# Weighting each token's row by two expert weights: input tiles of 22 tokens instead of 24, output tiles of half an input tile, and four-token VectorE products

## The chip, the cores and the metric

The kernel runs on one core of one Trainium2 chip. The metric is the device time of one execution in microseconds (us), the median of several runs. The profile is one execution recorded by the hardware profiler; its times are counted from the start of its span.

## What is computed

`x` holds 16 x 1024 = 16,384 tokens of 512 float32 values, `expert_weights` two float32 weights for each token. The output has, for each token, its row times the first weight and its row times the second. `expert_indices` is not used.

```
x_expanded = x[:, :, np.newaxis, :].repeat(k, axis=2)     # k = 2
weights = expert_weights[..., np.newaxis]
return (x_expanded * weights).astype(np.float32)
```

So 33.6 MB of `x` and 0.13 MB of weights are read and 67.1 MB are written, with one multiplication for each value written.

## The kernel before, in words

The 16,384 tokens are seen as 128 tokens for each of 128 partitions. `groups` cuts these 128 into input tiles of 24 tokens a partition five times and 8 once. In a tile of T tokens, partition p holds T neighbouring tokens, so its share of `x` is one contiguous run of T x 2 KB in memory and its share of the output one of T x 4 KB. One token a partition is 128 x 2 KB = 0.26 MB of `x` and 0.52 MB of output.

There are three pools: one tile for all the weights, two buffers for input tiles (`x_pool`, 48 KB a partition each) and two for output tiles (`o_pool`, 12 tokens, 48 KB a partition each).

- **Weights** (lines 53, 54 and 58): three transfers issued by SyncE (SP) at the start, for the first tile, the other four tiles of 24, and the last tile.
- **Loads** (`load`, line 82): issued on ScalarE's (ACT's) queue. Tile 0 comes in six pieces of 4 tokens, so that work can begin early; the others are one transfer each. `load(0)` and `load(1)` are issued before the loop; `load(i + 2)` stands behind the products of tile i, since it writes the buffer that they read.
- **Products** (lines 100 and 106): for each token and each of its two weights one instruction of 128 x 512 values. Of three successive ones, two run on VectorE (DVE, `tensor_scalar`, line 106) and one on ACT (`mul`, line 100).
- **Stores** (line 115): issued by SP when 12 tokens, one output tile of 6.29 MB, are multiplied; 11 stores in all, the last of 8 tokens. The output tile can be written again when its store has landed, so the products of one output tile wait for the store two before it.

The order on each engine is the order in the source. Waits are put in by the framework: a product waits for its input tile or piece and for its output buffer; a store on SP waits for the products of both engines; `load(i + 2)` on ACT's queue waits for DVE's products of tile i, and ACT's next products stand behind it. A transfer's packets are spread over the core's 16 DMA engines, 8 rows (partitions) of a tile to each engine; each row of a tile is one packet.

Of the kernel before, what the change touches and what calls it, by code (L numbers as in the profile page):

```python
# [1 line left out]

# [4 lines left out]


@with_exitstack
def kernel(  # L10
    ctx: ExitStack,
    tc: tile.TileContext,
    x: bass.AP,
    expert_indices: bass.AP,
    expert_weights: bass.AP,
    out: bass.AP,
):
    nc = tc.nc

    batch, seq, hidden = x.shape  # L20
    k = expert_weights.shape[-1]
    P = nc.NUM_PARTITIONS
    ntok = batch * seq
    assert ntok % P == 0
    A_TOTAL = ntok // P

    f32 = mybir.dt.float32
    row = k * hidden
    TX = 24
    TO = 12  # L30

    groups = [[24], [24], [24], [24], [24], [8]]
    assert sum(sum(g) for g in groups) == A_TOTAL

    xf = x.rearrange("b s h -> (b s) h")
    of = out.rearrange("b s k h -> (b s) (k h)")
    wf = expert_weights.rearrange("b s k -> (b s) k")

    w_pool = ctx.enter_context(tc.tile_pool(name="w_pool", bufs=1))
    x_pool = ctx.enter_context(tc.tile_pool(name="x_pool", bufs=2))  # L40
    o_pool = ctx.enter_context(tc.tile_pool(name="o_pool", bufs=2))

    w_tile = w_pool.tile([P, A_TOTAL * k], f32)

    def rows(of_all, done, T):
        return of_all[done * P : (done + T) * P, :].rearrange(
            "(p a) n -> p (a n)", a=T
        )

    T0 = sum(groups[0])  # L50
    G = len([g for g in groups[1:] if sum(g) == T0])
    head = (1 + G) * T0
    nc.sync.dma_start(out=w_tile[:, : T0 * k], in_=rows(wf, 0, T0))
    nc.sync.dma_start(
        out=w_tile[:, T0 * k : head * k].rearrange("p (g n) -> p g n", g=G),
        in_=wf[T0 * P : head * P, :].rearrange("(g p a) n -> p g (a n)", g=G, p=P),
    )
    nc.sync.dma_start(
        out=w_tile[:, head * k :], in_=rows(wf, head, A_TOTAL - head)
    )  # L60

    tiles = []
    done = 0
    for group in groups:
        T = sum(group)
        a0 = 0
        for n in group:
            tiles.append((done, T, a0, n))
            a0 += n
        done += T  # L70

    loaded = []

    def load(i):
        if i >= len(tiles):
            return
        done, T, a0, n = tiles[i]
        x_tile = x_pool.tile([P, TX * hidden], f32)
        src = rows(xf, done, T)
        step = TX // 6 if i == 0 else n  # L80
        for at in range(0, n, step):
            nc.scalar.dma_start(
                out=x_tile[:, at * hidden : (at + step) * hidden],
                in_=src[:, (a0 + at) * hidden : (a0 + at + step) * hidden],
            )
        loaded.append(x_tile)

    for i in range(2):
        load(i)
    for i, (done, T, a0, n) in enumerate(tiles):  # L90
        x_tile = loaded[i]
        outr = rows(of, done, T)
        for t in range(n):
            if t % TO == 0:
                o_tile = o_pool.tile([P, TO * row], f32)
            for kk in range(k):
                c = (done + a0 + t) * k + kk
                o = t % TO * row + kk * hidden
                if c % 3 == 2:
                    nc.scalar.mul(  # L100
                        out=o_tile[:, o : o + hidden],
                        in_=x_tile[:, t * hidden : (t + 1) * hidden],
                        mul=w_tile[:, c : c + 1],
                    )
                    continue
                nc.vector.tensor_scalar(  # L106
                    out=o_tile[:, o : o + hidden],
                    in0=x_tile[:, t * hidden : (t + 1) * hidden],
                    scalar1=w_tile[:, c : c + 1],
                    scalar2=None,  # L110
                    op0=mybir.AluOpType.mult,
                )
            if (t + 1) % TO == 0 or t + 1 == n:
                at = t // TO * TO
                nc.sync.dma_start(  # L115
                    out=outr[:, (a0 + at) * row : (a0 + t + 1) * row],
                    in_=o_tile[:, : (t + 1 - at) * row],
                )
        load(i + 2)

# [1 line left out]
_INS = ['x', 'expert_indices', 'expert_weights']  # L122
_OUTS = [((16, 1024, 2, 512), 'float32')]


# [23 lines left out]
```

## Time and profile before

| What | Value |
|---|---|
| median of 3 runs | 240.81 us (240.47, 240.81, 240.90) |
| span of the profiled execution | 238.9 us |
| median less that span | 1.9 us |
| DVE busy | 69.0 us, 171 instructions |
| ACT busy | 54.9 us, 86 instructions |
| data moved | 100.81 MB, 422 GB/s over the span |
| stores issued | 10 of 6144 KB and one of 4096 KB |
| loads issued | 6 of 1024 KB, 4 of 6144 KB, one of 2048 KB |

The profiled execution's own time outside the profiler is not recorded for this kernel, only its span. What lies around the span is therefore taken as the difference to the median, 1.9 us. The busy times say how long an engine's instructions ran; an engine that is idle most of the time waits for something, and the profile names what released it. The row of DMA shares says which part of the time the 16 DMA engines were moving packets.

### The profile page before, as it was taken

The page shows a single profiled execution, that of the slowest core. Times are in us where ns is not written, and L with a number is a line of the kernel's source. Part 1 is how long each engine was busy: PE and PEld are TensorE (multiplying, and loading weights), DVE is VectorE, ACT ScalarE, POOL GpSimd, SP SyncE. Part 2 cuts the span into 40 slices and gives each one's busy share as a digit, 9 for nine tenths or more (in the row PEclk, how much of TensorE's full clock was granted, in tenths as well). Part 3 has the DMA queues.
Part 4 walks back from the last instruction along what each step waited for, and adds up shares of the span by engine and source line. Part 5 has one row for each costly group of instructions (what it writes and reads, how often), then busy time and mean ns, then how long its engine had stood idle before and what let it go on. Part 6 is the DMA issues. An engine that isn't in the chain of part 4 may idle for free.

```text
span 238.9 us, 364 instructions
## 1 busy us (share of the span) xinstructions
DVE 69.0 (29%) x171; ACT 54.9 (23%) x86; POOL 0.2 (0%) x4
## 2 busy tenths in 40 slices
DVE  0890300004609100190063037003706406415000
ACT  0870300004308000170071034003406106213000
POOL 0000000000000000000000000000000000000000
DMA  6999999999999999999999999999989899999994
GB/s 244 420 443 395 495 395 395 494 428 395 428 494 395 413 494 411 395 446 469 403 411 502 395 420 453 436 411 428 469 379 496 381 428 469 436 411 428 436 439 197
DMA packets 3986, 100.81 MB, mean 422 GB/s; under 512 B 1168, under 2 KB 1168, under 8 KB 1168
## 3 DMA queue, kind: packets, MB, share of 16 engines
q1 hardware_dynamic: 2400, 67.24, 65.2%
q10 hardware_dynamic: 1584, 33.56, 33.1%
q14 instruction: 2, 0.02, 0.0%
HBM read 33.69 MB, written 67.11 MB: 422 GB/s over the span
## 4 chain that ended last, share of the span: by engine, by line
DMA 66%; DVE 13%; another core or an unknown queue 11%; issue 0%; DVEq 0%; SPq 0%
DMA out_dram<-o_tile 54%; DVE o_tile L106 13%; DMA x_tile<-in_x_dram 11%; DVEq L144 0%; DVEq L106 0%; SPq L115 0%
## 5 line engine op out<-in xcount | busy, mean ns | idle before, releaser
L106 DVE TENSOR_SCALAR o_tile<-x_tile,w_tile 128x512 f32<-128x512 f32 x171 | 69.0, 480 | 149.3 <-DMA out_dram<-o_tile 105.3
L100 ACT ACTIVATE o_tile<-x_tile,w_tile 128x512 f32<-128x512 f32 x85 | 53.6, 709 | 155.5 <-DMA out_dram<-o_tile 116.8
L100 ACT ACT_TABLE_LOAD x1 | 1.3, 1283 | 6.7 <-DMA x_tile<-in_x_dram 6.7
L133 POOL MEMSET const-bfloat16-1.0<- 128x1 bf16 x1 | 0.1, 101 | 0.0
L133 POOL MEMSET const-uint8-127<- 128x1 uint8 x1 | 0.1, 101 | 0.0
L133 POOL MEMSET const-float32-0.0<- 128x1 f32 x1 | 0.1, 98 | 0.2 <-issue 0.2
L133 POOL MEMSET const-float32-1.0<- 128x1 f32 x1 | 0.1, 98 | 0.0
## 6 DMA issues: line engine op xcount, KB each, us to landing
out_dram<-o_tile SPq DMA_DIRECT2D x10, 6144.0 KB, 33.6
x_tile<-in_x_dram ACTq DMA_DIRECT2D x4, 6144.0 KB, 43.9
x_tile<-in_x_dram ACTq DMA_DIRECT2D x6, 1024.0 KB, 10.6
out_dram<-o_tile SPq DMA_DIRECT2D x1, 4096.0 KB, 19.5
x_tile<-in_x_dram ACTq DMA_DIRECT2D x1, 2048.0 KB, 24.0
w_tile<-in_expert_weights_dram SPq DMA_DIRECT2D x1, 96.0 KB, 11.1
w_tile<-in_expert_weights_dram SPq DMA_DIRECT2D x1, 24.0 KB, 2.9
w_tile<-in_expert_weights_dram SPq DMA_DIRECT2D x1, 8.0 KB, 13.2
```

Of the source, the lines that this page charges most:

```text
L100: nc.scalar.mul(out=o_tile[:, o : o + hidden], in_=x_tile[:, t * hidden : (t + 1) * hidden], mul=w_tile[:, c : c + 1],)
L106: nc.vector.tensor_scalar(out=o_tile[:, o : o + hidden], in0=x_tile[:, t * hidden : (t + 1) * hidden], scalar1=w_tile[:, c : c + 1], scala ...
L133: nc = _bacc.Bacc("TRN2", target_bir_lowering=False, num_devices=1)
```

## The change

- Input tiles are 22 tokens five times and 18 once. The buffers shrink to 44 KB a partition.
- Each output tile is half of its input tile: 11 tokens and 11, or 9 and 9 for the last. The first half of every tile uses one buffer (`o_pool0`), the second half the other (`o_pool1`). There are 12 stores: ten of 11 tokens (5.77 MB) and two of 9 (4.72 MB).
- Tile 0 comes in pieces of 4, 4, 3, 5, 4 and 2 tokens. The weights' three transfers stand between the first pieces in the source; they are still issued by SP and the pieces by ACT.
- The first half of tile 0 is multiplied as before, one instruction for each token and weight, 15 on DVE and 7 on ACT. In every other half, tokens 0 to 3 are one DVE `tensor_tensor` (4 tokens x 2 weights x 512 = 4096 values a partition, with both inputs broadcast by a step of zero), tokens 4 to 7 are eight ACT products, and the rest (3 tokens, 3072 values; in the last tile 1 token, 1024 values) another DVE `tensor_tensor`.
- `LAST` is 0, so the branches that it guards do nothing.

DVE has 15 products and 22 `tensor_tensor` instructions instead of 171 products; ACT has 95 products instead of 85.

```diff
-    TX = 24
-    TO = 12
-    groups = [[24], [24], [24], [24], [24], [8]]
+    groups = [22, 22, 22, 22, 22, 18]
+    TX = max(groups)
...
-    o_pool = ctx.enter_context(tc.tile_pool(name="o_pool", bufs=2))
+    o_pools = [
+        ctx.enter_context(tc.tile_pool(name=f"o_pool{h}", bufs=1)) for h in range(2)
+    ]
...
-        step = TX // 6 if i == 0 else n
-        for at in range(0, n, step):
+        steps = [4, 4, 3, 5, 4, 2] if i == 0 else [n]
+        for e, step in enumerate(steps):
+            at = sum(steps[:e])
             nc.scalar.dma_start(
...
+            if i == 0 and e < 3:
+                weights(e)
...
+    def product(engine, o_tile, t, x_in, c, m):
+        o = t * row
+        if engine is not None:
+            for e in range(m * k):
...
+                if engine is nc.scalar or engine is nc.any and (c + e) % 3 == 2:
+                    nc.scalar.mul(out=out_e, in_=in_e, mul=w_e)
+                else:
+                    nc.vector.tensor_scalar(
...
+            return
+        nc.vector.tensor_tensor(
+            out=o_tile[:, o : o + m * row].rearrange(
+                "p (t k h) -> p t k h", t=m, k=k
+            ),
+            in0=x_in[:, : m * hidden]
+            .rearrange("p (t h) -> p t h", t=m)
+            .unsqueeze(2)
+            .to_broadcast([P, m, k, hidden]),
+            in1=w_tile[:, c : c + m * k]
+            .rearrange("p (t k) -> p t k", t=m)
+            .unsqueeze(3)
+            .to_broadcast([P, m, k, hidden]),
+            op=mybir.AluOpType.mult,
+        )
...
+        for h, (at, to) in enumerate([(0, (n + 1) // 2), ((n + 1) // 2, n)]):
+            m = to - at
+            o_tile = o_pools[h].tile([P, (TX + 1 - h) // 2 * row], f32)
+            cuts = list(range(0, min(m, 2 * CH) + 1, CH)) + [m] * (m > 2 * CH)
+            for e, (t, u) in enumerate(zip(cuts, cuts[1:])):
+                if i == 0 and h == 0:
+                    engine = nc.any
+                else:
+                    engine = nc.scalar if e == 1 else None
+                product(
...
+            nc.sync.dma_start(
+                out=outr[:, at * row : to * row], in_=o_tile[:, : m * row]
+            )
         load(i + 2)
```

## Prediction, on record before the changed kernel ran

> **What bounds the kernel now.** I read the page's DMA rows first, because DVE and ACT are busy less than a third of the span.
>
> ```profile
> DMA  6999999999999999999999999999989899999994
> GB/s 244 420 443 395 495 395 395 494 428 395 428 494 395 413 494 411 395 446 469 403 411 502 395 420 453 436 411 428 469 379 496 381 428 469 436 411 428 436 439 197
> ...
> q1 hardware_dynamic: 2400, 67.24, 65.2%
> q10 hardware_dynamic: 1584, 33.56, 33.1%
> ```
>
> The 16 DMA engines have work in every slice but the first and the last. Stores (q1) and loads (q10) took 65.2 + 33.1 = 98.3% of their time: 234.9 us of 238.9. About 4 us are idle, and the next view, the busy time in chosen stretches, shows where.
>
> ```profile
> 0.00:2.00 2.00, 0.00 (x0) 0.00 (x0) 0.20 (x4) 1.00 0.19 29
> 2.00:6.00 4.00, 0.15 (x1) 0.00 (x0) 0.00 (x0) 1.00 0.93 354
> 6.00:30.00 24.00, 12.92 (x32) 11.61 (x17) 0.00 (x0) 1.00 1.06 436
> 30.00:60.00 30.00, 2.90 (x8) 2.94 (x6) 0.00 (x0) 1.00 0.98 423
> 60.00:125.00 65.00, 20.17 (x52) 15.85 (x27) 0.00 (x0) 1.00 1.00 434
> 125.00:143.00 18.00, 4.48 (x12) 3.14 (x7) 0.00 (x0) 1.00 1.01 437
> ...
> 237.00:238.90 1.90, 0.00 (x0) 0.00 (x0) 0.00 (x0) 1.00 0.00 0
> ```
>
> The last two columns are DMA share and GB/s. Before 2 us nothing has arrived, and from 237 us on nothing moves; in between the rate is 423 to 437 GB/s, whether loads and stores are mixed (60 to 125 us) or only stores run (125 to 143 us). A stretch books a packet where it starts, so single stretches scatter around the mean. 100.81 MB at 434 GB/s are 232.3 us; the two ends and the run-in are the other 6.6.
>
> Last, the stores' own pace, from the end of the timeline.
>
> ```profile
> 199.35 5.01 ACT L100 ACTIVATE o_tile<-x_tile,w_tile 128x512 f32<-128x512 f32 x8 [13.02 <-DMA out_dram<-o_tile]
> 199.45 6.42 DVE L106 TENSOR_SCALAR o_tile<-x_tile,w_tile 128x512 f32<-128x512 f32 x16 [11.67 <-DMA out_dram<-o_tile]
> 205.94 12.84 SPq L115 DMA_DIRECT2D out_dram<-o_tile  x2
> 213.91 3.17 ACT L100 ACTIVATE o_tile<-x_tile,w_tile 128x512 f32<-128x512 f32 x5 [9.55 <-DMA out_dram<-o_tile]
> ```
>
> ACT is released by a landed store at 199.35 us and by the next at 213.91: 14.56 us for 6.29 MB, 432 GB/s, with no pause between the stores. DVE needs 6.42 us for its 16 products of an output tile, then idles. The bound is the movement of bytes. Compute matters only if it comes so late that the DMA engines run dry.
>
> **The change, part by part.**
>
> *Tile sizes.* The bytes are the same. Loads have 768 + 5 x 128 = 1,408 row packets before and after; stores go from 11 x 128 to 12 x 128, 8 packets more on each DMA engine. In the trace's packet records a 48 KB packet took 1.815 us and a 32 KB one 1.213; the line through both leaves 1.213 - 2 x (1.815 - 1.213) = 0.009 us for a packet of no bytes. That is 8 x 0.009 = 0.07 us. Rows of 44 and 36 KB lie between sizes that both move at full pace. Cost: +0.1 us.
>
> *One more store.* 12 completions instead of 11. Each is covered by the store or load queued behind it: the 14.56 us above are 8 packets of 1.815 us, 14.52, so 0.04 us are left between two stores. I take 0.0; with no cover I bound it by the 1.3 us that lie between the last packet record (237.6 us) and the span's end. [...]
>
> *Products.* After the change, a half has 4096 + 3072 = 7168 values on DVE and eight products on ACT. ACT needs 5.01 us, as now. No `tensor_tensor` is in the trace. The lower bound is the pace of DVE's products, 6.42 us / (16 x 512) = 0.78 ns a value, 5.6 us a half; the upper is the slowest row, one ACT product's 709 ns / 512 = 1.38 ns, 9.9 us. I take 7.7 us, half way, since the second input is the reason to be slower than the first row and the engine the reason to be faster than the second. [...]
>
> *What covers it.* The tightest place is where no load is in flight and one store runs while the other output tile is computed. A store of 11 tokens then takes 14.56 x 11/12 = 13.3 us. From it go 1.1 us from an issue to its first packet (first load issued at 0.73 us, first packet record at 1.84) and 0.2 for waits and issue: 12.0 us for the products. The DMA engines finish a store up to 1.8 us apart (packet records), so the first of them has 10.2. Even 9.9 us fits; so 0.0. If the cover is gone, each late us is paid once for each output tile in such a place. Waits of DVE on stores with no load due (before: between 115 and 128, 161 and 172, and from 195 us on) come to about six.
>
> *Load issue.* `load(i + 2)` waits on ACT's queue for DVE, some 1.3 us longer than now (7.7 against 6.42). ACT's next products are queued behind it; they need a landed store first (waits of 9.55 to 24 us), so nobody is delayed. The DMA engines still have a store queued. 0.0; uncovered it would be 1.3 us for each of four loads.
>
> *Start.* Three pieces, 11 tokens, make the first output tile, instead of 12 tokens. Issue was at 13.38 us. SP's first store may come some 0.5 us earlier, but loads of tiles 0 and 1 (11.5 MB, 26 us) keep the DMA engines occupied. The weights' place in the source moves nothing: SP waits for nothing there, and its three issues end at 2.1 us either way. 0.0, between -0.3 and +0.3 (the run-in of 2 to 6 us, at 354 GB/s, loses 4 x (1 - 354/434) = 0.7 us).
>
> *End.* The last products are those of 9 tokens; they need 5120 values on DVE (at most 7.1 us by the slowest row) under a store of 9 tokens, 10.9 us. After them only stores run, as now, and the idle 1.9 us behind 237 us stay. 0.0.
>
> **Sum:** 238.9 + 0.1 = 239.0 us of span; with the 1.9 us between span and median, **240.9 us**. The three runs before span 0.43 us, so about 0.2% is what can be told from no change.
>
> **Rivals.**
>
> *DVE starves the DMA engines (slower).* If a value of the double broadcast takes over 12.0 us / 7168 = 1.67 ns, stores in the places named come late. At 13 us a half: six times 1.0, 246.9. For it: such an instruction is nowhere in the trace, and its second input has a step of zero within 512 values. Against it: even the slowest row gives 9.9. Chance 0.05.
>
> *A cost for each store or row size (slower).* If one more completion is not covered, or rows of 44 KB move 0.5% slower than those of 48 KB, 1.1 to 1.3 us come on top: 242.1. For it: 48 KB rows are all that the long stages show. Against it: 32, 16 and 48 KB rows all move at 27 GB/s an engine. Chance 0.07.
>
> *The ends shrink (faster).* The DMA engines end 1.8 us apart (235.8 to 237.6 us); were they level, the last would end 0.9 us earlier: 240.0. For it: the last store starts from another phase of loads and stores, and the engines have fewer instructions around it. Against it: each DMA engine carries the same bytes before and after. Chance 0.10.
>
> *The change does not do what it says*, a half that is not in flight with the other: the two buffers alternate as before, and no wait is added, so nothing would follow from it either.
>
> **Chances and range.** Forecast, within 0.2% (240.3 to 241.3): 0.64. Beyond it upward: 0.05 + 0.07 + 0.08 for scatter of the run-in and between runs = 0.20. Downward: 0.10 + 0.06 for the same scatter = 0.16. The range takes in the shrunken ends and the cost for each store, 240.0 to 242.1; starvation stays outside.
>
> **What would show it.** Right: DMA slices of 9 from the second to the last but one, DVE idle before nearly every half for a landed store, 13.3 us between the last releases by 11-token stores, `tensor_tensor` rows between 3.2 and 5.7 us for 4096 values. Wrong: a slice of 8 or less in a stage of stores alone, stores waiting on DVE there, or a rate under 430 GB/s between 60 and 200 us.

## The result and the profile after

The changed kernel takes 242.6 us (242.47, 242.61 and 242.79) against 240.75 (240.47 to 240.90, 4 runs): a ratio of 1.0076, 95% interval 1.0061 to 1.0090. It is slower, by 1.9 us; 240.9 was forecast, and the range ended at 242.1. One more execution took 250.1 us; in all, 20 of the 95 executions of kernels with 22-token tiles and none of the 144 with 24-token tiles (without e4 below, which has most products left out) were slow outliers, most at 248 to 253 us, which are left out of every comparison and whose cause no run shows.

The span of the profiled execution is 240.5 us instead of 238.9. The page of the changed kernel has these DMA rows:

```profile
DMA  6999999998999999989999899999999999999993
GB/s 241 420 401 481 398 465 412 442 457 382 465 435 420 457 390 450 459 382 472 420 427 472 360 472 420 427 465 398 424 436 430 424 465 427 420 432 435 441 411 135
...
q1 hardware_dynamic: 2544, 67.24, 64.9%
q10 hardware_dynamic: 1584, 33.56, 33.0%
```

The DMA engines are occupied in the same way: (64.9 + 33.0)% of 240.5 us are 235.4, against 234.9 before. So 0.5 us of the loss is packet time, and the rest is idle. No slice between the ends is under 8 (three are 8, two before); the last has fallen from 4 to 3 and from 197 to 135 GB/s. The busy time by stretches of the changed kernel (DMA share and GB/s last) places it:

```profile
60.00:125.00 65.00, 24.20 (x7) 15.03 (x24) 0.00 (x0) 1.00 1.00 431
125.00:150.00 25.00, 7.70 (x2) 5.01 (x8) 0.00 (x0) 1.00 1.00 429
150.00:205.00 55.00, 23.46 (x7) 15.43 (x25) 0.00 (x0) 1.00 1.01 437
...
230.00:236.00 6.00, 0.00 (x0) 0.00 (x0) 0.00 (x0) 1.00 0.94 406
236.00:237.00 1.00, 0.00 (x0) 0.00 (x0) 0.00 (x0) 1.00 0.26 111
237.00:238.00 1.00, 0.00 (x0) 0.00 (x0) 0.00 (x0) 1.00 0.26 111
```

And the end of the kernel before, in the same stretches:

```profile
230.00:236.00 6.00, 0.00 (x0) 0.00 (x0) 0.00 (x0) 1.00 0.99 426
236.00:237.00 1.00, 0.00 (x0) 0.00 (x0) 0.00 (x0) 1.00 0.08 33
237.00:238.00 1.00, 0.00 (x0) 0.00 (x0) 0.00 (x0) 1.00 0.00 0
```

Compute is not late: the DMA share is 1.00 or more in these stretches from 60 to 205 us. After 236 us a share of 0.26, some four of the 16 DMA engines, still starts packets in the changed kernel, and hardly any did before. (A packet is booked where it starts: the last four start between 236.89 and 237.85 us and end between 238.26 and 239.22.) The packet records give when the DMA engines end (each transfer closes with 16 packets of 4 bytes, in the changed kernel 240 for the 15 transfers of SP's queue and 176 for the 11 of ACT's; I take one for each DMA engine):

| | first ends | last ends | apart | mean of 16 | span |
|---|---|---|---|---|---|
| before | 235.84 | 237.64 | 1.80 | 236.45 | 238.94 |
| changed | 235.84 | 239.22 | 3.38 | 236.80 | 240.49 |

The first ends at the same moment. The last is 1.58 us later, and the span is 1.55 us longer. In the changed kernel four end between 238.3 and 239.2, the other twelve by 236.7. That is where the loss lies; what makes the four late is the question of the experiments.

The records tell a little more. A packet's usual time follows from its size (1.815 us for 48 KB, 1.665 for 44). From 18 us on, 24 of the 640 load packets and 7 of the stores' took over 0.08 us longer, 9.7 us in sum over the 16 DMA engines; before it was 6 and 5, 3.3 us. Nearly all such long packets lie where loads and stores run together. Of the 94 load packets that had, averaged over their time, 6 to 12 store packets in flight beside them, 19 were long; of 183 such before, 3. Where only stores run, from 205 us on, there is none in either kernel. Joined into chains, each start to the nearest end, four chains hold 8.8 of 10.5 us of excess time after 17.5 us (3.3, 2.8, 1.4 and 1.3), so few DMA engines seem to bear it. The records do not name the DMA engine, and chains that meet can be exchanged: the chain with 3.3 us ends at 236.3, not late, and has 181 large packets where an even share is 184. So this much is an inference.

The two-input products themselves, by shape:

```profile
L125 DVE TENSOR_TENSOR o_tile<-x_tile,w_tile 128x4096 f32<-128x4096 f32 x11 | 48.7, 4425 | 119.1 <-DMA out_dram<-o_tile 97.4 <-DMA x_tile<-in_x_dram 21.7
L125 DVE TENSOR_TENSOR o_tile<-x_tile,w_tile 128x3072 f32<-128x3072 f32 x9 | 30.2, 3352 | 11.6 <-DMA x_tile<-in_x_dram 11.6
```

and the last releases by stores:

```profile
191.24 5.01 ACT L115 ACTIVATE o_tile<-x_tile,w_tile 128x512 f32<-128x512 f32 x8 [17.76 <-DMA out_dram<-o_tile]
191.34 7.69 DVE L125 TENSOR_TENSOR o_tile<-x_tile,w_tile 128x4096 f32<-128x4096 f32 x2 [15.13 <-DMA out_dram<-o_tile]
204.60 5.01 ACT L115 ACTIVATE o_tile<-x_tile,w_tile 128x512 f32<-128x512 f32 x8 [8.35 <-DMA out_dram<-o_tile]
204.62 5.56 DVE L125 TENSOR_TENSOR o_tile<-x_tile,w_tile 128x4096 f32<-128x4096 f32 x2 [5.59 <-DMA out_dram<-o_tile]
217.91 5.01 ACT L115 ACTIVATE o_tile<-x_tile,w_tile 128x512 f32<-128x512 f32 x8 [8.29 <-DMA out_dram<-o_tile]
```

DVE needs 7.69 us for a half and then waits for a store; from one release to the next are 13.3 us.

### The profile page after: what moved, and what is told of

It is laid out like the page before. It is cut to its first block, busy times and chain, and to the rows that moved or that the text cites. A ratio compares the mean times of both kernels' runs of the same rounds, so it can differ in the third digit from the quotient of the medians.

```text
span 240.5 us, 246 instructions
## 1 busy us (share of the span) xinstructions
DVE 86.6 (36%) x37; ACT 60.9 (25%) x96; POOL 0.2 (0%) x4
## 3 DMA queue, kind: packets, MB, share of 16 engines
q1 hardware_dynamic: 2544, 67.24, 64.9%
## 4 chain that ended last, share of the span: by engine, by line
DMA 76%; DVE 13%; issue 4%; DVEq 1%; SPq 0%
DMA out_dram<-o_tile 64%; DVE o_tile L125 13%; DMA x_tile<-in_x_dram 12%; DVEq L196 0%; DVEq L125 0%; SPq L162 0%
## 5 line engine op out<-in xcount | busy, mean ns | idle before, releaser
L125 DVE TENSOR_TENSOR o_tile<-x_tile,w_tile 128x4096 f32<-128x4096 f32 (+2 forms) x22 | 80.5, 3695 | 130.8 <-DMA out_dram<-o_tile 97.4
L115 ACT ACTIVATE o_tile<-x_tile,w_tile 128x512 f32<-128x512 f32 x95 | 59.6, 709 | 155.4 <-DMA out_dram<-o_tile 119.6
L117 DVE TENSOR_SCALAR o_tile<-x_tile,w_tile 128x512 f32<-128x512 f32 x15 | 6.2, 482 | 6.1 <-DMA x_tile<-in_x_dram 6.1
```

The lines of the kernel that those rows point to most:

```text
L115: nc.scalar.mul(out=out_e, in_=in_e, mul=w_e)
L117: nc.vector.tensor_scalar(out=out_e, in0=in_e, scalar1=w_e, scalar2=None, op0=mybir.AluOpType.mult,)
L125: nc.vector.tensor_tensor(out=o_tile[:, o : o + m * row].rearrange("p (t k h) -> p t k h", t=m, k=k), in0=x_in[:, : m * hidden] .rearrange ...
```

## The experiments

My theory after the result: the last DMA engine sets the end, and some get longer packets while loads and stores are mixed ("mixing", at first "phase"). Its rivals: the rows of 44 KB are slower as such ("rows"); the two-input products slow packets that pass while they run ("products").

Each ratio is to the kernel before on the same chip; the kernels ran on several chips.

| kernel | median, us | ratio to before, 95% interval |
|---|---|---|
| changed | 242.61 | 1.0076 (1.0061 to 1.0090) |
| e1: its tiling, single-token products | 242.34 | 1.0056 (1.0029 to 1.0083) |
| e2: tiling of before, four-token products | 241.18 | 1.0022 (1.0011 to 1.0034) |
| e5: changed, one queue | 242.22 | 1.0050 (1.0028 to 1.0071) |
| e6: before, one queue | 243.77 | 1.0132 (1.0107 to 1.0156) |
| e7: before, last piece of 2 | 240.80 | 1.0006 (0.9994 to 1.0018) |
| e8: changed, last piece of 4 | 240.93 | 1.0020 (0.9997 to 1.0042) |
| f1: changed, again | 241.91 | 1.0056 (1.0041 to 1.0070) |
| f4: e1 with last piece of 4 | 240.91 | 1.0023 (1.0006 to 1.0040) |
| g1: changed, last piece of 3 | 241.52 | 1.0037 (1.0022 to 1.0052) |
| g2: changed, last piece of 6 | 240.76 | 1.0013 (0.9995 to 1.0031) |
| g3: e2 with last piece of 2 | 241.32 | 1.0023 (1.0002 to 1.0045) |
| g4: changed, piece of 2 issued fourth | 241.62 | 1.0037 (1.0018 to 1.0056) |

### One half of the change at a time

e1, the changed tiling with the products of before:

```diff
-                if i == 0 and h == 0:
-                    engine = nc.any
-                else:
-                    engine = nc.scalar if e == 1 else None
+                engine = nc.any
```

> The changed tiling (22 tokens five times and 18, halves, 12 stores) with the products of before in every half: one instruction for each token and weight, two of three on VectorE. Theory rows (the layout with rows of 44 and 36 KB makes some packets slow on some DMA engines, which then end late): 242.4 to 242.9 us, the last landing over 3 us behind the first. Theory products (the four-token instructions, which read two inputs, slow packets that pass while they run): 240.5 to 241.0. Theory chance of phase (any new timing shifts who is late): anywhere from 240.5 to 243, with no order.

e2, the tiling of before with the products of the change:

```diff
-    groups = [22, 22, 22, 22, 22, 18]
+    groups = [24, 24, 24, 24, 24, 8]
...
-        steps = [4, 4, 3, 5, 4, 2] if i == 0 else [n]
+        steps = [4, 4, 4, 4, 4, 4] if i == 0 else [n]
...
-        for h, (at, to) in enumerate([(0, (n + 1) // 2), ((n + 1) // 2, n)]):
+        for h, (at, to) in enumerate([(0, 12), (12, 24)] if n == 24 else [(0, n)]):
```

> The tiling, the pieces and the 11 stores of before, with four-token VectorE instructions and eight ScalarE products in each output tile but the first. Theory rows: 240.5 to 241.0 us. Theory products: 242.4 to 242.9. Theory phase: anywhere between.

The tiling alone costs 0.56%, from 240.58 to 243.13 us in eight executions; the products alone 0.22%, 0.5 us, more than theory rows left for them. By the medians the tiling carries most of the loss, though the two intervals meet. Theory products falls as the main cause. Theory rows passes here within 0.1 us, but the scatter of e1, 2.5 us with nothing changed between its executions, speaks for a matter of how the DMA engines fall into step. That is an argument, not yet a test.

### Transfers with the products left out

e3 and e4 fill the two output tiles with zeros once and compute two products for each store:

```diff
+    nc.gpsimd.memset(o_tiles[0], 0.0)
+    nc.vector.memset(o_tiles[1], 0.0)
...
+            o_tile = o_tiles[h]
+            for kk in range(k):
+                c = (done + to - 1) * k + kk
+                nc.vector.tensor_scalar(
+                    out=o_tile[:, kk * hidden : (kk + 1) * hidden],
+                    in0=x_tile[:, (to - 1) * hidden : to * hidden],
...
```

> The changed tiling and all of its transfers, with nearly all products left out: each half is filled once with zeros at the start, and only its last token's two products are computed into its first row before each store. Theory rows: 242.4 to 242.9 us, since the transfers are the same. Theory products: 240.5 to 241.0. Theory phase: anywhere between.

> The tiling and transfers of before, with nearly all products left out in the same way. Theories rows and products: 240.5 to 241.0 us, as before. Theory phase: it differs from the kernel before by up to 2 us, although neither rows nor the kind of products changed.

e3 took 241.7 us once and 248.1 to 250.5 us five times, and answers nothing. e4, with the rows and transfers of before, took 250.1 to 251.3 us in all five. In its profile the mixed stretch is slow, the stretch of stores is not, and most DMA engines end late:

```profile
30.00:60.00 30.00, 0.88 (x2) 0.00 (x0) 1.00 1.00 395
60.00:90.00 30.00, 0.88 (x2) 0.00 (x0) 1.00 1.01 415
...
130.00:200.00 70.00, 3.53 (x8) 0.00 (x0) 1.00 1.00 432
...
240.00:248.00 8.00, 0.00 (x0) 0.00 (x0) 1.00 0.34 147
```

At 30 to 60 us the DMA engines are occupied (share 1.00) and move 395 GB/s; from 130 to 200 us 432. The DMA engines end from 236.7 to 247.1 us, nine of them after 244. No theory had expected a loss of 10 us, and its cause is not shown. What it shows is the same picture, larger, with no two-input product and no 44 KB row.

### Loads and stores in one queue

In e5 (changed) and e6 (before) SP issues the loads too. While loads are still queued, whole transfers then pass in turn: the stores' releases of DVE come alternately 13.3 to 13.5 and 26.5 to 27.2 us after the one before in e5 (44.77 to 165.84 us), the time of one and of two transfers of 5.77 MB at 432 GB/s (13.4 and 26.7); in e6, with 6.29 MB, 14.4 to 14.5 and 29.1 to 30.0 (50.30 to 196.93 us).

```diff
-            nc.scalar.dma_start(
+            nc.sync.dma_start(
                 out=x_tile[:, at * hidden : (at + step) * hidden],
```

> The changed kernel with its loads issued on SP too, so that loads and stores stand in one queue and each DMA engine takes them one after the other, in place of a load packet and a store packet in turn. Theory mixing (some DMA engines take longer packets in stretches where loads and stores alternate, and end late): hardly a long packet, landings of one store under 2 us apart, 240.3 to 240.9 us. Theory rows (44 KB rows as such): it stays at 242.4 to 242.9.

> The kernel before with its loads on SP too. Theory mixing: the same as the 22-token kernel with one queue within 0.3 us, 240.2 to 240.8. Theory rows: 240.5 to 240.9, 1.5 us or more under the 22-token kernel with one queue.

Both expectations failed. e6 starts late by an oversight: its three weight transfers are issued ahead of the first load on the same queue. Its run-in, against 354 GB/s before:

```profile
2.00:6.00 4.00, 0.00 (x0) 0.00 (x0) 0.00 (x0) 1.00 0.80 238
```

The first load is issued at 2.18 us instead of 0.73, so some 1.5 of its 3.2 us are that. The rest is again the spread at the end: by the packet records its DMA engines end between 237.24 and 240.82 us, 3.58 apart against 1.80 before.

```profile
236.00:242.00 6.00, 0.00 (x0) 0.00 (x0) 0.00 (x0) 1.00 0.29 126
```

So in one queue 24-token tiles, whose long rows are of 48 KB, end further apart than the 22-token tiles of e5 (3.0). e5 shows no such delay and still is at 242.2. Its landings tell where the DMA engines drift apart: in turn, the loads of tiles 2 to 5 land with 0.87, 1.52, 2.07 and 3.02 us between the first and the last DMA engine, and each pair of stores in between keeps the spread of the load before it. (Before the load of tile 2 it was 0.7.) Of its 38 long packets, 32 lie at the ends of loads (28, 68, 108, 149 and 187 us). So alternating packet by packet is not needed: with one queue the DMA engines end 3.0 us (e5) and 3.58 us (e6) apart, with two 3.38 (changed). In e5 the spread came with the loads that passed among stores, and not with those at the start (0.7 us) or with the stores.

### The tilings with few loads

f2 (changed) and f3 (before) leave out the loads of tiles 2 to 5 and multiply tiles 0 and 1 again, so that from some 50 us on only stores run.

```diff
+        if i >= 2:
+            loaded.append(loaded[i % 2])
+            return
```

> The changed kernel with the loads of tiles 2 to 5 left out; their products read the tiles 0 and 1 again, all 12 stores and the products stay. 67.1 + 2 x 5.77 = 78.6 MB, at 434 GB/s 181.2 us, with 6.6 for the ends and 1.9 around the span 189.7. Theory mixing: 189.2 to 190.2, and after the last load (some 45 us) no packet over 0.1 us too long, the spread of the landings stays as it is then. Theory rows (or a hidden cost for each store): 190.8 or more, and the spread grows along the stores.

> The kernel before with the loads of tiles 2 to 5 left out in the same way: 67.1 + 2 x 6.29 = 79.7 MB, 183.6 us, with 8.5 around it 192.1. Theory mixing: 191.6 to 192.6, so that both tilings lie at their bytes over the same rate within 0.5 us. Theory rows: at its sum, while the 22-token kernel lies 1 us or more above its own.

f3 is the changed source with e2's tiling, e1's products and pieces of 4. They took 192.5 and 194.5 us, 2.8 and 2.4 above their sums (f2 so in the range of theory rows, f3 outside both ranges), for a reason that I had not counted: with no load behind tile 1, the DMA engines run dry once while its halves are multiplied. The stretches of f2 show it (54 to 60 us):

```profile
54.00:60.00 6.00, 6.00 (x3) 4.45 (x9) 0.00 (x0) 1.00 0.35 150
60.00:66.00 6.00, 6.00 (x2) 3.06 (x6) 0.00 (x0) 1.00 1.12 481
```

By the packet records 3.0 us are idle there in f2 and 2.8 in f3. Without them both profiles are within 0.5 us of the sum: 190.4 - 3.0 = 187.4 against 187.8, and 192.9 - 2.8 = 190.1 against 190.2 (the sums less the 1.9 outside the span). Then the stores, first f2's of 11 tokens, then f3's of 12:

```profile
74.11 5.01 ACT L118 ACTIVATE o_tile<-x_tile,w_tile 128x512 f32<-128x512 f32 x8 [11.05 <-DMA out_dram<-o_tile]
...
87.47 5.01 ACT L118 ACTIVATE o_tile<-x_tile,w_tile 128x512 f32<-128x512 f32 x8 [8.34 <-DMA out_dram<-o_tile]
```

```profile
80.26 5.01 ACT L118 ACTIVATE o_tile<-x_tile,w_tile 128x512 f32<-128x512 f32 x8 [12.24 <-DMA out_dram<-o_tile]
...
94.81 5.01 ACT L118 ACTIVATE o_tile<-x_tile,w_tile 128x512 f32<-128x512 f32 x8 [9.54 <-DMA out_dram<-o_tile]
```

13.36 us for 5.77 MB and 14.55 for 6.29 are 432 GB/s each. Over the seven full stores from there on, by their landings, it is 13.39 and 14.59 us a store, 431 GB/s each. The spread of the landings is 0.7 us or less in both from there to the end. So where only stores run a row of 44 KB costs nothing as such, nor does one more store: theory rows falls, as far as stores alone can tell. That 44 KB rows cost something only beside loads is not tested apart; e6 shows that they are not needed for the spread.

### The pieces of the first tile

When the first store starts, the last pieces of tile 0 are still queued, and small load packets and large store packets then pass in turn. In the changed kernel 110 small packets were left at that moment (16.0 us) and passed until 27.9 us, while 109 store packets started; in the kernel before 64 (17.0 us), until 25.9 us beside 71. e7 gives the kernel before a last piece of 2 tokens, e8 the changed kernel one of 4 (in this order; both are edits of the changed source, and e7 has e2's tiling and e1's products besides):

```diff
-        steps = [4, 4, 3, 5, 4, 2] if i == 0 else [n]
+        steps = [4, 4, 4, 4, 6, 2] if i == 0 else [n]
...
-        steps = [4, 4, 3, 5, 4, 2] if i == 0 else [n]
+        steps = [4, 4, 3, 4, 3, 4] if i == 0 else [n]
```

> The kernel before, its tiling and products, with the first tile's pieces of 4, 4, 4, 4, 6 and 2 tokens, so that the last piece is one of 4 KB packets as in the changed kernel. Theory mixing, if the last piece sets the phase in which the DMA engines alternate: away from 240.7 by 0.5 us or more, likely 241.5 to 243. If the piece sets nothing, or by theory rows: 240.4 to 241.0.

> The changed kernel with pieces of 4, 4, 3, 4, 3 and 4 tokens, so that the last piece has 8 KB packets as in the kernel before. Theory mixing with the last piece as what sets the phase: back towards 240.7, under 241.8. If the piece sets nothing, or by theory rows: 242.4 to 242.9.

e8 comes back to 1.0020: 49 small packets are left, and its end in the stretches is

```profile
230.00:236.00 6.00, 0.00 (x0) 0.00 (x0) 0.00 (x0) 1.00 0.95 412
236.00:237.00 1.00, 0.00 (x0) 0.00 (x0) 0.00 (x0) 1.00 0.01 0
```

with the DMA engines 1.02 us apart. It has 32 long load packets, more than the 24 of the changed kernel, though its long packets lose less in sum (7.9 us, loads and stores, against 9.7), and by their chains they are spread over the DMA engines, none over 1.2 of 8.6 us: what seems to count is whether few bear them. e7, with 131 small packets left, stays at 1.0006, so the piece alone does nothing that the medians show to 24-token tiles with single-token products.

Next I ran the changed kernel again beside e1's products with the last piece of 4 (f4), and then, since the cause was still open, four more: the changed kernel with a last piece of 3 (g1) and of 6 (g2), e2 with e7's pieces (g3), and the pieces as changed but with that of 2 issued fourth (g4). The edits of g1, g2 and g4:

```diff
-        steps = [4, 4, 3, 5, 4, 2] if i == 0 else [n]
+        steps = [4, 4, 3, 5, 3, 3] if i == 0 else [n]
...
+        steps = [4, 4, 3, 5, 6] if i == 0 else [n]
...
+        order = [0, 1, 2, 5, 3, 4] if i == 0 else [0]
...
+            step = steps[order[e]]
+            at = sum(steps[: order[e]])
```

> The changed kernel itself, unaltered, on the same chip as the three others. If its loss belongs to the kernel: 242.0 to 243.0 us in most runs. If it hangs on how the DMA engines fall into step in a given run: a spread of over 1.5 us between runs, as the changed tiling with single-token products showed (240.6 to 243.1).

> The changed tiling with the single-token products of before and first pieces of 4, 4, 3, 4, 3 and 4 tokens. If a last piece of 4 tokens is what brings the changed kernel back to 241.2, whatever the products: 240.6 to 241.6. If not: 242 to 243, as with the last piece of 2.

> The changed kernel with first pieces of 4, 4, 3, 5, 3 and 3 tokens. Theory first overlap (how many small load packets are still queued when the first store starts sets how far the DMA engines fall out of step): between the last piece of 2 (242.6) and of 4 (241.2), 241.2 to 242.2 us. Theory chance (any timing gives another pattern, the piece has no order): no place between the two.

> The changed kernel with five first pieces of 4, 4, 3, 5 and 6 tokens, so no small one at the end. Theory first overlap: fewest small packets left, 240.6 to 241.4 us. Theory chance: may lie anywhere from 240.6 to 243.

> The tiling and stores of before, four-token products, first pieces of 4, 4, 4, 4, 6 and 2. Theory first overlap: as many small packets left as with the changed kernel, so 241.8 to 243. The single-token products with these pieces stayed at 240.8, so if the tile size has to come with it: 240.9 to 241.5.

> The changed kernel with the same pieces of 4, 4, 3, 5, 4 and 2 tokens, the piece of 2 issued fourth, so that a piece of 4 is last in the queue. Theory first overlap: as with a last piece of 4, 240.8 to 241.8 us. If the split of the tokens matters and not the order of the packets: 242.0 to 242.8.

The changed kernel is slower here too, by 0.56% (241.70, 241.91 and 242.50), though two of the three are under the 242.0 that was expected. With 22-token tiles the ratio falls as the last piece grows: 1.0076 and 1.0056 with 2 tokens, 1.0037 with 3, 1.0020 and 1.0023 with 4, 1.0013 with 6 (110, 58, 49 or 42, and 30 small packets left). Neighbours overlap, the ends do not. By order alone (g4) it is 1.0037, between 2 and 4, in the range of the first expectation, though its interval overlaps that of f1. But g4 has 44 small packets left, as many as the kernels with a last piece of 4, so their count alone does not order the kernels. g3, with 130 left, has e2's median (1.0023 and 1.0022), but not its executions: six lie between 240.5 and 241.0 us and six between 241.6 and 242.2, where eleven of e2's twelve lie between 240.9 and 241.3. So with four-token products it stays open what the piece does to 24-token tiles.

In every one of the 18 profiles the span is the last DMA engine's end and 1.2 to 1.6 us. Some of them:

| | last ends | apart | span |
|---|---|---|---|
| e8 | 237.09 | 1.02 | 238.3 |
| g2 | 237.52 | 1.51 | 238.7 |
| e2 | 237.87 | 1.87 | 239.1 |
| e5 | 238.94 | 3.02 | 240.2 |
| g3 | 238.99 | 2.87 | 240.2 |
| e1 | 239.59 | 3.70 | 241.2 |
| e6 | 240.82 | 3.58 | 242.1 |

In the twelve that load all tiles, without e3, e4, e6 and f1, the first DMA engine ends between 235.8 and 236.3 us. The profile of g3 is one of its six longer executions, and there 24-token tiles end 2.9 us apart.

## Why the prediction was wrong

- *One more store and the row sizes* (0.0 and 0.1 us): right where only stores run. f2 moves its 11-token stores at the pace of f3's 12-token ones, 432 GB/s each.
- *Products* (7.7 us a half): 7.69 measured. That the half-way point between two bounds hit it is luck. That a second input makes DVE slower was my estimate; measured are 7.69 us for 7168 values, 1.07 ns a value, against the 0.78 of the single-token products. The three sizes in the trace, 1,218 ns for 1024 values, 3,352 for 3072 and 4,425 for 4096, give by an estimate 1.04 ns a value and some 0.15 us for each instruction. The lower bound that I set from DVE's present pace was not reached.
- *What covers it* (0.0): right. No stretch shown from 60 to 205 us is under a share of 1.00, and DVE waits for a store 5.6 us or more in the stretch of stores. Starvation was no cause. That the four-token products alone still cost 0.5 us (e2) is not explained by a late half, since e2's DMA slices stay at 8 and 9 between the ends.
- *Start* (0.0 within 0.3): the first store was issued 1.0 us earlier (12.39 us), and the DMA engines stayed occupied, as said. What I missed is the other consequence: which load packets were still queued beside the first store changed, and from e8, g1 and g2 that is worth up to 1.5 us with this tiling, or 1.0 measured from f1.
- *End* (0.0): this is the step that failed. I read that the DMA engines end 1.8 us apart and took this for a fixed property of the end ("the idle 1.9 us behind 237 us stay"); the rival on it was that it shrinks. It grew to 3.4 us, and the 1.58 us by which the last DMA engine ends later are the 1.55 us of the span. The rate before, 434 GB/s in mixed stretches as in stretches of stores, hid it, because it is a mean over 16 DMA engines. One of the two stretches was misread as well: of 125 to 143 us only the part up to 131.6 has stores alone, since the load issued at 127.86 us moves packets from there on. By the packet records the pace that I read off holds all the same: 117 to 128 us, with stores alone, has 434 GB/s.
- *What would show it*: nearly all the signs of being right came, DVE's waits for stores, the 13.3 us between releases and the `tensor_tensor` times, while the time was wrong, since none of them looks at how far apart the DMA engines end. The one sign of being wrong that came, a rate under 430 GB/s (429 at 125 to 150 us), is no evidence: the kernel before has 429 in a stretch too (171 to 187 us).
- *The range* reached 242.1 through a cost for each store or row size that stretches of stores alone do not show. A rival "the DMA engines end further apart" would have had its price from the same table: here 1.58 us more on the last of them were 1.55 us of the span.

Shown: the place of the loss (the end, on four DMA engines), no cost of the 44 KB rows or the twelfth store without mixed loads, and that with 22-token tiles the pieces of the first tile alone, with nothing else changed, take most of the loss away. By the medians only: the tiling as its larger part, and the order from a last piece of 2 to one of 6. Still open: why some packets take longer and, by the chains, few DMA engines seem to bear them (8.8 of 10.5 us on four chains), why the products alone cost 0.5 us, and why 24-token tiles with single-token products are indifferent to the piece.

## What to carry to other kernels

In all 18 profiles the span ended 1.2 to 1.6 us behind the last DMA engine's end, and in the two kernels compared here the DMA engines ended 1.8 and 3.4 us apart at nearly the same mean rate (422 and 419 GB/s): when transfers set the time, look at how far apart the DMA engines end, not only at the mean rate. A change that leaves the bytes and the cover alone can still shift which load packets pass beside which stores; here, by the medians, the pieces of the first tile alone were worth 1.0 to 1.5 us of 240, and the whole change 1.9. A forecast of "no change" needs a margin for it on the slow side. With the 22-token tiles the small transfers still queued when the large stream started were part of it (ratios of 1.0056 and 1.0076 with 110 small packets left, 1.0013 with 30), so that is a place to look first.

## What the runs showed of the hardware beyond that

- While the first store and the last pieces of tile 0 were both queued, the two queues shared the DMA engines packet by packet. In the changed kernel the 110 small load packets left, 6.9 for each DMA engine, took from 16.0 to 27.9 us: 1.7 us each, about the time of one 44 KB store packet, although one of 4 KB itself is recorded with 0.16 us, a tenth of that. The store packets start there in rounds of 16, from 16.01, 17.83 and 19.65 us, 1.82 us apart: 1.665 for 44 KB and 0.159 for 4 KB. In the kernel before the rounds are 2.12 us apart (from 16.97, 19.09 and 21.21 us): 1.815 for 48 KB and 0.309 for 8 KB.
- In e5 the DMA engines drew apart from 0.7 to 3.0 us over the four loads that passed among stores; loads alone at the start left them 0.7 to 0.8 us apart there, and stores alone, in f2 and f3, never more than 0.7. Stores alone kept the spread that they met: in each of the last five stores of the changed kernel (first landings from 187 to 236 us) the last DMA engine lands 3.38 us after the first, in each of the last four of the kernel before 1.80.
